# A fused two-layer trunk on one core: PSUM banks of the mLSTM given out anew, its sums of squares taken behind the products of the values, and in the tail the sums of squares one half later

## The chip, the cores and the metric

The kernel runs on one core of one Trainium2 chip. The metric is the device time of one execution in microseconds (us); the median of three runs of the kernel before is 1196.1 us (1193.45 to 1197.48). One more execution was taken under the hardware profiler; all rows of the trace are from that one.

## The reference, cut to what matters

The input is 512 tokens of 1024 channels in float32. Two layers follow each other, and a last norm.

```python
def rmsnorm(x, g):
    y = x * lax.rsqrt(jnp.mean(x * x, axis=-1, keepdims=True) + EPS)
    return y * g

def sqrelu_mlp(h, w1, w2):
    return jnp.square(jax.nn.relu(h @ w1)) @ w2

# layer 0
h = h + diff_attention(rmsnorm(h, attn_norm[0]), ...)
h = h + sqrelu_mlp(rmsnorm(h, mlp_norm[0]), w1[0], w2[0])     # 1024 -> 4096 -> 1024
# layer 1
h = h + mlstm_mixer(rmsnorm(h, mlstm_norm[0]), ...)
h = h + sqrelu_mlp(rmsnorm(h, mlp_norm[1]), w1[1], w2[1])
return rmsnorm(h, final_norm)

def mlstm_mixer(h, ...):
    proj = h @ w_in            # q and k (512 + 512), v 1024, output gate 1024, gates 8
    qk = silu(causal_depthwise_conv(q and k, width 4))
    i_pre, log_f = gates       # 4 heads each; log_sigmoid of the second
    ...                        # scores, decays, values of 4 heads, rmsnorm of each head
    return (sigmoid(o_pre) * ht) @ w_out
```

## The kernel before, in words

Everything lies with channels on the 128 partitions and the 512 tokens along a row: the residual stream is `h[0]` to `h[7]` (two of them in one tile, `h2[0]` to `h2[3]`). A product in float32 is made of three matmuls: each operand is split in a rounded high part (`hi`, ScalarE, `L254`) and the rest (`lo`, VectorE, `L528`; `L513` for the operands of the layers), and `hi*hi`, `lo*hi` and `hi*lo` are summed in PSUM. Weights come in units of 128 rows by 1024 columns: SyncE starts a DMA into one of three `raw` tiles, ScalarE writes `whi`, VectorE writes `wlo`; a unit is requested two units ahead of its use. The MLP's second product goes by a Strassen-like scheme of seven products (`down`, `L922` to `L924`), whose sums are taken out of PSUM by `L937` to `L940` and added to `h` by `L945`.

**Order.** TensorE's instructions stand in the order in which the Python code emits them. Each step of a matrix product calls `tick`, and `after(n, fn)` puts a piece of side work (a norm, a head's scores) `n` ticks behind the place where it is called, so the `T_...` numbers say where in TensorE's order side work stands. On VectorE, ScalarE and GpSimdE a scheduler orders the instructions as the program is built. All engines run their own list strictly in order.

**PSUM** has 8 banks of 512 columns. `idle` holds them with the one that was given out longest ago first. `banks(mm=3, sc=2, ac=3)` gives the first 3 to the tag `mm`, the next 2 to `sc` and the last 3 to `ac`, in the order in which the call names the tags. `bank(tag)` takes a tag's banks in turn.

**The start of the mLSTM.** While `down` for the last rows of `h` (`q` = 3, `i` = 3) is being taken out of PSUM, `mlstm` begins: `vpair_mm(x, 264)` makes the values of head 0 with the gates, 256 + 8 columns, for four blocks of 128 tokens in four banks (one of `mm`, three of `ac`), over eight operands `x[0]` to `x[7]`: 96 matmuls, `L432` to `L434`, 16 ticks. The operands come from `h` by ScalarE (`xh`) and VectorE (`xl`). The norm's factor for each token comes from the sum of squares over the channels: `square_in` squares each `h[k]` (ScalarE) and adds the squares to `acc` (GpSimdE, `L524`); `token_scale`, `T_MRS` ticks after the start, splits `acc`, sums over the partitions by two matmuls (`L535`, `L536`), and takes the reciprocal root: `L559`, then Ln, Exp and Square on ScalarE, then `L552`, `L553` and `L561`, which writes `rs`. `T_GATES` ticks behind the 96 matmuls, `gates` turns `rs` (`L569`), reads the gates (`L1047`, `L1049`) and takes the values out of their four banks (ScalarE, and VectorE's `L582`). Eight tiles of q and k follow (`ntile_mm`, n0 to n7 here: 24 matmuls of 512 columns each, 8 ticks, `L400` to `L402`), which go into the `mm` banks in turn, and are taken out by `evict_qk`: `L1026`, one ScalarE pass, three `L1030` on VectorE, a sigmoid, `L1035` or `L1037`, a split. `T_GROWS` and `T_GCOLS` place the work on the gates' rows and columns. Ln and Exp lie in one of ScalarE's function tables and the sigmoid in another; changing it is `L245`. Then come the heads: their scores are `L1106` (decays) and `L1117` to `L1119`, both in the two `sc` banks.

**The tail.** `finish` makes the last two rows of tiles of the output, `h[6]` and `h[7]` (`j` = 0, 1), for the first 256 tokens and then for the other 256 (`i` = 0, 1): 24 matmuls for each `j` and `i`. `early_sums` splits `acc` (squares of `h[0]` to `h[5]`) and sums it over the partitions by four matmuls, `L1249` and `L1250`; `tail` adds the product to `h` (`L1256`) and squares it; `scaled` adds those two squares (`L1262`), takes the reciprocal root, multiplies `h` by it (`L1272`) and starts the DMAs to the output. The last norm's weights and a factor of -0.5 are put on `h` beforehand (`L1253`, `L1258`).

Of the kernel before, what the change touches and what calls it, by code (L numbers as in the profile page):

```python
# [14 lines left out]
AF = mybir.ActivationFunctionType  # L15
ALU = mybir.AluOpType
# [6 lines left out]
KT = D // P  # L23
# [11 lines left out]
C_AN, C_M0, C_MN, C_M1, C_FN, C_HN, C_SUB, C_CW, C_CB = 0, 8, 16, 24, 32, 40, 48, 49, 81  # L35
# [22 lines left out]
T_M, T_H = 15, 22  # L58
D_MLS = [(5, 8, 6), (5, 7, 9), (5, 9, 10), (7, 8, 12)]

T_GATES, T_GROWS, T_GCOLS, T_MRS = 3, 22, 56, 9
T_SIG = 2

T_MLP = 11
# [121 lines left out]
def trunk(ctx: ExitStack, tc, xT, wgt, wgt2, cols, rows, rel, consts, outT):  # L186
# [18 lines left out]
    def banks(**tags):  # L205

        free = list(idle)
        for tag, n in tags.items():
            turn[tag], free = free[:n], free[n:]
# [15 lines left out]
    mm = nc.tensor.matmul  # L225
    vec = nc.vector
    pool = nc.gpsimd
# [22 lines left out]
    def act(out, x, func, **kw):  # L250
        name = {AF.Exp: LNSET, AF.Ln: LNSET, AF.Sigmoid: SGSET}.get(func)
        if name:
            tables(name)
        ins = nc.scalar.activation(out, x, func, **kw)  # L254
        if name:
            behind(ins, loaded["load"])
            loaded["uses"].append(ins)
# [238 lines left out]
    def col(c):  # L496
        return colt[:, c : c + 1]
# [17 lines left out]
            square_in(k, acc)  # L515
        return lambda: (hi, lo)

    def square_in(k, acc):
        if k == 0:
            act(acc, h[k], AF.Square)  # L520
        else:
            s = tmp()
            act(s, h[k], AF.Square)
            pool.tensor_tensor(acc, acc, s, op=ALU.add)  # L524

    def split(src, hi, lo, eng=None):
        act(hi, src, AF.Copy)
# [35 lines left out]
    def scale_tile(name):  # L563
        return cp.tile([P, T], F32, tag=name, name=nm(name))
# [276 lines left out]
    def mlp(x, acc, g0, finish=None):  # L841
        with ExitStack() as st:
# [49 lines left out]
            def down(q, i):  # L892
# [53 lines left out]
                for n in (2 * i, 2 * i + 1):  # L946
                    if g0 is not None:
                        nxt.append(operand(n, g0, nacc))
                    else:
                        if n == 0:  # L950
                            finish.acc = acc_tile()
                        square_in(n, finish.acc)

            after(T_MLP, lambda: token_scale(acc, rs))
            ps = group_mm(x)
# [24 lines left out]

    def mlstm(x, acc):
        with ExitStack() as st:
            banks(mm=3, sc=2, ac=3)
            gp = Buffers(tc, st, name="gp", bufs=1)
            qp = Buffers(tc, st, name="qp", bufs=16)
            sg = Buffers(tc, st, name="sg", bufs=8)
# [248 lines left out]
    def finish(operands):  # L1235
# [10 lines left out]
        def early_sums():  # L1246
            split(acc, sh, sl)
            for s, c in zip(stat, (slice(0, H), slice(H, T))):
                mm(s[:, :H], ones_d, sh[:, c], start=True, stop=False)  # L1249
                mm(s[:, :H], ones_d, sl[:, c], start=False, stop=False)  # L1250

        for k in range(KT - 2):
            vec.tensor_scalar(h[k], h[k], col(C_FN + k), -0.5, op0=ALU.mult, op1=ALU.mult)  # L1253

        def tail(n, c, s):
            vec.tensor_tensor(h[n][:, c], part[n - pair[0]][:, c], h[n][:, c], op=ALU.add)  # L1256
            act(s, h[n][:, c], AF.Square)
            vec.tensor_scalar(h[n][:, c], h[n][:, c], col(C_FN + n), -0.5, op0=ALU.mult, op1=ALU.mult)  # L1258

        def scaled(c, stat, ss):  # L1260
            for s in ss:
# [16 lines left out]
        for i, c in enumerate((slice(0, H), slice(H, T))):  # L1278
            ss = [tmp()[:, :H] for _ in pair]
            for j, n in enumerate(pair):  # L1280
                hi, lo = units[j]
                for k in range(KT):
                    w = slice(k * P, (k + 1) * P)
                    a, b = operands(k, i)
                    mm(part[j][:, c], hi[:, w], a, start=k == 0, stop=False)
                    mm(part[j][:, c], hi[:, w], b, start=False, stop=False)
                    mm(part[j][:, c], lo[:, w], a, start=False, stop=k == KT - 1)
                    tick()
                tail(n, c, ss[j])
                if i == 0 and j == 0:  # L1290
                    early_sums()
            if i == 0:
                after(T_FIN, lambda c=c, ss=ss: scaled(c, stat[0], ss))
            else:
                scaled(c, stat[1], ss)
# [94 lines left out]
```

## Time and profile before

| | |
|---|---|
| median of 3 runs | 1196.1 us (1193.45 to 1197.48) |
| the profiled execution | 1194.34 us, of which the span from first to last instruction 1192.3 us |
| TensorE matmuls | 1147.5 us busy, 96% of the span |
| VectorE | 919.9 us, 77% |
| ScalarE | 603.0 us, 51% |
| GpSimdE | 189.2 us, 16% |
| granted TensorE clock, mean | 0.983 |

Reading: matmuls are pipelined, so each row's duration (0.28 us for 256 columns) is longer than the distance to the next one's start (0.12 us); the distance is what counts. A row of the timeline gives the start, the duration, the engine, the line, what is written and read, and in brackets how long the engine sat idle ahead of it and what released it. In the view by windows, each stretch has its length, then busy microseconds and instructions of TensorE's matmuls (PE), its weight loads, VectorE (DVE), ScalarE (ACT) and GpSimdE (POOL), the clock granted to TensorE as a share of full speed, the share of the DMA engines and what they moved.

### The profile page before, as it was taken

Reading aid. Unit: us, or ns where it says so; the run is one execution under the profiler, and the core shown is the slowest. Engines: PE = TensorE matmul, PEld = TensorE weight load, DVE = VectorE, ACT = ScalarE, POOL = GpSimd, SP = SyncE. Lnnn points to the kernel's source line nnn. Section 1 sums busy time; section 2 is a strip of 40 time slices with the busy share of each in tenths; the row PEclk is TensorE's granted clock in tenths of the full one; section 3 lists DMA queues with packets and bytes.
Section 4 is the critical chain, followed back from the end, with each engine's and each line's share of the span. In section 5 each row is a group of like instructions: output and inputs, shape, how many; then the busy total and the mean of one; then the engine's idle time right before and its main releaser. Section 6 shows DMA issues by size and latency. Waiting matters only on the chain.

```text
span 1192.3 us, 17221 instructions
## 1 busy us (share of the span) xinstructions
PE 1147.5 (96%) x6730; PEld 1011.2 (85%) x6730; DVE 919.9 (77%) x1387; ACT 603.0 (51%) x909; POOL 189.2 (16%) x180
## 2 busy tenths in 40 slices
PE   7899999999999999999989899999999999999994
PEld 5778888888998998989877789888889889899894
DVE  7789888587967957867989857766697686786884
ACT  5577776564534534434544537654453353443441
POOL 4432332130000000000221312223000000000011
PEclk9899999999999999999989999999999999999997
DMA  6622222233263362461222221223325526426312
GB/s 202 198 71 71 75 85 71 71 124 111 66 190 112 89 176 89 111 191 53 83 71 70 76 83 54 57 85 107 110 84 136 171 67 162 139 67 185 89 32 71
DMA packets 36592, 123.91 MB, mean 104 GB/s; under 512 B 4351, under 2 KB 6418, under 8 KB 36512
## 3 DMA queue, kind: packets, MB, share of 16 engines
q1 hardware_dynamic: 30288, 103.38, 27.0%
q0 software_dynamic: 5104, 17.87, 7.7%
q10 hardware_dynamic: 1120, 1.57, 0.4%
q8 instruction: 53, 0.87, 0.3%
q14 instruction: 27, 0.22, 0.1%
HBM read 108.11 MB, written 4.74 MB: 95 GB/s over the span
## 4 chain that ended last, share of the span: by engine, by line
PE 78%; DVE 14%; ACT 3%; issue 3%; DMA 2%; POOL 1%; DVEq 0%; SPq 0%; POOLq 0%; ACTq 0%
PE bank L401 15%; PE bank L402 15%; PE bank L400 15%; PE bank L923 7%; PE bank L924 7%; PE bank L922 7%; DVE wlo L528 2%; PE bank L432 2%; PE bank L433 1%; PE bank L434 1%; DVE tmp_tmp L1030 1%; DMA raw<-wgt 1%; DVE x_xl L513 1%; PE bank L730 1%; ACT whi L254 1%
## 5 line engine op out<-in xcount | busy, mean ns | idle before, releaser
L402 PE MATMUL bank<-x_xh,wlo 128*128 128x512 f32 x640 | 255.4, 399 | 1.3 <-DVE wlo L528 1.3
L401 PE MATMUL bank<-x_xl,whi 128*128 128x512 f32 x640 | 254.8, 398 | 1.0 <-DVE x_xl L513 1.0
L400 PE MATMUL bank<-x_xh,whi 128*128 128x512 f32 x640 | 254.0, 397 | 1.4 <-ACT whi L254 1.4
L254 ACT ACTIVATE whi<-raw 128x1024 fp32r<-128x1024 f32 (+2 forms) x128 | 133.4, 1042 | 120.9 <-PE bank L923 48.1
L528 DVE TENSOR_TENSOR wlo<-raw,whi 128x1024 fp32r<-128x1024 f32 (+2 forms) x128 | 161.9, 1265 | 35.2 <-ACT whi L254 34.6
L922 PE MATMUL bank<-uh,whi 128*128 128x256 f32 x560 | 157.9, 282 | 0.0
L924 PE MATMUL bank<-uh,wlo 128*128 128x256 f32 x560 | 157.8, 282 | 0.0
L923 PE MATMUL bank<-ul,whi 128*128 128x256 f32 x560 | 157.8, 282 | 0.0
L400 PEld LDWEIGHTS bank<-x_xh,whi 128*128 128x128 f32 x640 | 122.8, 192 | 28.8 <-ACT whi L254 2.1
L402 PEld LDWEIGHTS bank<-x_xh,wlo 128*128 128x128 f32 x640 | 121.1, 189 | 29.3 <-DVE wlo L528 2.4
L401 PEld LDWEIGHTS bank<-x_xl,whi 128*128 128x128 f32 x640 | 121.5, 190 | 28.3 <-DVE x_xl L513 1.4
L922 PEld LDWEIGHTS bank<-uh,whi 128*128 128x128 f32 x560 | 106.0, 189 | 0.1
L923 PEld LDWEIGHTS bank<-ul,whi 128*128 128x128 f32 x560 | 105.7, 189 | 0.3
L924 PEld LDWEIGHTS bank<-uh,wlo 128*128 128x128 f32 x560 | 105.8, 189 | 0.0
L943 POOL DMA_DIRECT2D h<-work x24 | 20.8, 866 | 511.1 <-DVE work L940 391.5
L254 ACT ACTIVATE uh<-chains 128x1792 fp32r<-128x1792 f32 (+1 forms) x35 | 55.6, 1590 | 57.8 <-DVE chains L883 57.7
L528 DVE TENSOR_TENSOR ul<-chains,uh 128x1792 fp32r<-128x1792 f32 (+1 forms) x35 | 66.0, 1886 | 23.7 <-ACT uh L254 23.4
L524 POOL TENSOR_TENSOR acc_acc<-acc_acc,tmp_tmp 128x512 f32<-128x512 f32 x33 | 54.6, 1654 | 170.8 <-ACT tmp_tmp L254 169.7
L432 PE MATMUL bank<-whi,x_xh 128*128 128x256 f32 (+1 forms) x256 | 73.9, 289 | 7.1 <-DVE work L939 5.7
L876 DVE SCALAR_TENSOR_TENSOR tmp_tmp<-bank,rs_rs 128x512 f32<-128x512 f32 x64 | 44.1, 689 | 45.9 <-PE bank L402 45.5
L254 ACT ACTIVATE whi<-wsums 128x1024 fp32r<-128x1024 f32 x47 | 49.8, 1059 | 51.5 <-PE bank L923 30.3
L433 PE MATMUL bank<-wlo,x_xh 128*128 128x256 f32 (+1 forms) x256 | 73.0, 285 | 0.0
(302 smaller groups left out, 2669.6 us busy)
## 6 DMA issues: line engine op xcount, KB each, us to landing
raw<-wgt SPq DMA_DIRECT2D x156, 512.0 KB, 3.7
rawx<-wgt SPq DMA_DIRECT2D x32, 512.0 KB, 4.2
h<-work POOLq DMA_DIRECT2D x24, 512.0 KB, 5.8
skew<-frd POOLq DMA_DIRECT2D x8, 320.0 KB, 7.3
bias_bias<-skew POOLq DMA_DIRECT2D x8, 256.0 KB, 3.1
outT<-h SPq DMA_DIRECT2D x6, 256.0 KB, 2.5
raw<-wgt SPq DMA_DIRECT2D x2, 528.0 KB, 3.6
h<-xT ACTq DMA_DIRECT2D x4, 256.0 KB, 4.9
```

The costliest lines, as they stand in the source:

```text
L254: ins = nc.scalar.activation(out, x, func, **kw)
L400: mm(ps, whi, x[0], start=first, stop=False)
L401: mm(ps, whi, x[1], start=False, stop=False)
L402: mm(ps, wlo, x[0], start=False, stop=last)
L432: mm(ps, xh, hi[:, c], start=k == 0, stop=False)
L433: mm(ps, xh, lo[:, c], start=False, stop=False)
L524: pool.tensor_tensor(acc, acc, s, op=ALU.add)
L528: (eng or vec).tensor_tensor(lo, src, asf(hi), op=ALU.subtract)
L876: vec.scalar_tensor_tensor(m, p, 0.0, rs, op0=ALU.max, op1=ALU.mult)
L922: mm(out[name], hi[:, n], uh[:, t], start=first, stop=False, skip_group_check=late)
L923: mm(out[name], hi[:, n], ul[:, t], start=False, stop=False, skip_group_check=late)
L924: mm(out[name], lo[:, n], uh[:, t], start=False, stop=k == 3, skip_group_check=late)
```

## The change

Four edits:

1. The mLSTM's banks are given out in the order `ac`, `mm`, `sc` instead of `mm`, `sc`, `ac`.
2. Four places in the mLSTM's start: `token_scale` 22 ticks after the start instead of 9, `gates` 14 ticks behind the 96 matmuls instead of 3, the rows at 30 instead of 22, the columns at 60 instead of 56.
3. In the tail, `early_sums` stands behind the second `j` of the first half instead of the first, and the squares of `h[4]` and `h[5]` are added to `acc` by VectorE instead of GpSimdE.
4. Also in the tail, the weights of the last norm times -0.5 are made once (`gain`), and `h[0]` to `h[5]` are scaled by them on ScalarE instead of VectorE.

```diff
-T_GATES, T_GROWS, T_GCOLS, T_MRS = 3, 22, 56, 9
+T_GATES, T_GROWS, T_GCOLS, T_MRS = 14, 30, 60, 22
...
-    def square_in(k, acc):
+    def square_in(k, acc, eng=None):
         if k == 0:
             act(acc, h[k], AF.Square)
         else:
             s = tmp()
             act(s, h[k], AF.Square)
-            pool.tensor_tensor(acc, acc, s, op=ALU.add)
+            (eng or pool).tensor_tensor(acc, acc, s, op=ALU.add)
...
-                        square_in(n, finish.acc)
+                        square_in(n, finish.acc, vec if i == 2 else pool)
...
-            banks(mm=3, sc=2, ac=3)
+            banks(ac=3, mm=3, sc=2)
...
+        gain = scale_tile("rs2")[:, :KT]
+        vec.tensor_scalar(gain, colt[:, C_FN : C_FN + KT], -0.5, None, op0=ALU.mult)
         for k in range(KT - 2):
-            vec.tensor_scalar(h[k], h[k], col(C_FN + k), -0.5, op0=ALU.mult, op1=ALU.mult)
+            act(h[k], h[k], AF.Copy, scale=gain[:, k : k + 1])
...
-            vec.tensor_scalar(h[n][:, c], h[n][:, c], col(C_FN + n), -0.5, op0=ALU.mult, op1=ALU.mult)
+            vec.tensor_scalar(h[n][:, c], h[n][:, c], gain[:, n : n + 1], None, op0=ALU.mult)
...
-                if i == 0 and j == 0:
+                if i == 0 and j == 1:
                     early_sums()
```

Below are three places of the built programs, with the engine's instructions in their order. Lines from 1253 on have numbers larger by 2 in the changed kernel.

First, TensorE at the start of the 96 matmuls of `vpair_mm` (the four blocks of tokens go in four banks; the names end in the bank's number, 77 to 84). The first matmul of each block before:

```order
L432 MATMUL bank_80<-whi_91,x_xh_129 128x264
L432 MATMUL bank_84<-whi_91,x_xh_129 128x264
L432 MATMUL bank_82<-whi_91,x_xh_129 128x264
L432 MATMUL bank_83<-whi_91,x_xh_129 128x264
```

and of the change:

```order
L432 MATMUL bank_77<-whi_91,x_xh_129 128x264
L432 MATMUL bank_80<-whi_91,x_xh_129 128x264
L432 MATMUL bank_81<-whi_91,x_xh_129 128x264
L432 MATMUL bank_79<-whi_91,x_xh_129 128x264
```

VectorE's `L937` to `L940` of the last `down` read banks 84, 83 and 82 in both kernels; those now go to `mm`'s last place and to `sc`.

Second, ScalarE from the split of `acc` for the mLSTM's norm on (`sh` is the high part of `acc`, `chains` the tile of Ln, Exp and Square, `whi` a weight unit's high part, `vh` the values', `tmp<-conv` the first pass of `evict_qk`). Before:

```order
L254 ACTIVATE sh_sh_332<-acc_acc_128 128x512
L254 ACTIVATE whi_91<-raw_88 128x1024
L254 ACTIVATE chains<-chains 128x512 x3
L254 ACTIVATE whi_89<-raw_86 128x1024
L254 ACTIVATE vh_0_v_5227<-bank_80,rscol_rscol_472 128x256
```

and of the change:

```order
L254 ACTIVATE sh_sh_332<-acc_acc_128 128x512
L254 ACTIVATE whi_89<-raw_86 128x1024
L254 ACTIVATE chains<-chains 128x512
L254 ACTIVATE whi_90<-raw_87 128x1024
L254 ACTIVATE chains<-chains 128x512
L245 ACT_TABLE_LOAD
L254 ACTIVATE chains<-chains 128x512
L254 ACTIVATE tmp_tmp_255<-conv_5080,colt 128x512
L254 ACTIVATE vh_0_v_5276<-bank_77,rscol_rscol_472 128x256
```

The three passes of the reciprocal root now have a split of weights and a change of table between them; the table is changed 10 times in the whole program instead of 8 (the first load apart).

Third, the tail on VectorE, from the last step of `down` that it takes out of PSUM on (`h_96` is `h[2]` and `h[3]`, `h_97` is `h[4]` and `h[5]`, `h_98` is `h[6]` and `h[7]`). Before:

```order
L937 TENSOR_TENSOR work<-bank_80,work 128x2x256
L1253 TENSOR_SCALAR h_96<-h_96,colt 128x512
L938 TENSOR_TENSOR work<-bank_82,work 128x512
L939 TENSOR_TENSOR work<-bank_81,work 128x512
L940 TENSOR_TENSOR work<-bank_82,work 128x256
L945 TENSOR_TENSOR h_97<-h_97,work 128x1024
L1256 TENSOR_TENSOR h_98<-bank_78,h_98 128x256
L1253 TENSOR_SCALAR h_97<-h_97,colt 128x512 x2
L1258 TENSOR_SCALAR h_98<-h_98,colt 128x256
L528 TENSOR_TENSOR sl_sl_333<-acc_acc_128,sh_zeros 128x512
```

and of the change:

```order
L937 TENSOR_TENSOR work<-bank_77,work 128x2x256
L938 TENSOR_TENSOR work<-bank_81,work 128x512
L939 TENSOR_TENSOR work<-bank_78,work 128x512
L940 TENSOR_TENSOR work<-bank_81,work 128x256
L945 TENSOR_TENSOR h_97<-h_97,work 128x1024
L1258 TENSOR_TENSOR h_98<-bank_83,h_98 128x256
L524 TENSOR_TENSOR acc_acc_128<-acc_acc_128,tmp_tmp_204 128x512
L524 TENSOR_TENSOR acc_acc_128<-acc_acc_128,tmp_tmp_233 128x512
L1260 TENSOR_SCALAR h_98<-h_98,rs_0_rs_336_2325 128x256
L528 TENSOR_TENSOR sl_sl_333<-acc_acc_128,sh_zeros 128x512
```

The six scalings have left VectorE, and two adds have come. On TensorE the four matmuls of `early_sums` stood behind 24 matmuls of the first half, and now stand behind 48.

## The prediction, made before the run

> **What bounds the kernel now.** I read the page first, then who waited for whom on TensorE, then the stretches around its long waits.
>
> ```profile
> span 1192.3 us, 17221 instructions
> PE 1147.5 (96%) x6730; PEld 1011.2 (85%) x6730; DVE 919.9 (77%) x1387; ACT 603.0 (51%) x909; POOL 189.2 (16%) x180
> ```
>
> TensorE (PE) is busy for 96% of the span, so time is gained only where it stands still or runs slowly. Its waits (in all, times, longest):
>
> ```profile
> PE bank L432 <- DVE work L939: 5.7, 1, 5.7
> PE bank L1249 <- ACT sh_zeros L254: 5.1, 1, 5.1
> PE bank L1106 <- ACT e_e L254: 3.9, 1, 3.9
> ```
>
> The first is the start of the mLSTM, the second the tail, the third lies 80 us behind the first, where the heads' scores begin. The change touches the first two. In the view by windows each of them costs more than the wait:
>
> ```profile
> 593.11:596.52 3.41, 1.61 (x12) 1.19 (x10) 3.28 (x4) 2.88 (x5) 0.44 (x1) 1.00 0.64 234
> 596.52:606.76 10.24, 4.90 (x22) 4.90 (x23) 10.14 (x16) 2.92 (x6) 4.69 (x4) 0.50 0.28 90
> 606.76:610.17 3.41, 3.41 (x29) 3.41 (x28) 2.74 (x5) 1.34 (x2) 1.62 (x1) 1.00 0.00 0
> 1163.28:1166.69 3.41, 0.00 (x0) 0.00 (x0) 3.12 (x3) 1.16 (x4) 2.82 (x2) 0.98 0.00 0
> 1166.69:1173.52 6.83, 6.19 (x27) 5.89 (x28) 0.69 (x1) 0.45 (x1) 0.00 (x0) 0.51 0.00 0
> ```
>
> The granted clock falls to 0.50 after the wait and stays there for three and for two stretches of 3.41 us. Ahead of the first fall TensorE had been busy for 1.61 of 3.41 us: half a stretch of idleness is enough here. The second row also shows VectorE (DVE) busy for 10.14 of 10.24 us while TensorE waits. That decides what the first wait is worth.
>
> **The tail (edits 3 and 4).** In order of time, as now:
>
> ```profile
> 1157.07 1.27 DVE L1253 TENSOR_SCALAR h<-h,colt 128x512 f32<-128x512 f32 x3
> 1159.05 0.28 PE L1285 MATMUL bank<-uh,whi 128*128 128x256 f32 x1
> 1160.49 0.69 DVE L939 TENSOR_TENSOR work<-bank,work 128x512 f32<-128x512 f32 x1
> 1161.55 1.22 DVE L945 TENSOR_TENSOR h<-h,work 128x1024 f32<-128x1024 f32 x1
> 1161.79 0.28 PE L1287 MATMUL bank<-uh,wlo 128*128 128x256 f32 x1
> 1162.80 1.46 ACT L254 ACTIVATE tmp_tmp<-h 128x512 f32<-128x512 f32 x3 [4.46 <-DVE h L945]
> 1163.57 2.90 POOL L524 TENSOR_TENSOR acc_acc<-acc_acc,tmp_tmp 128x512 f32<-128x512 f32 x2 [2.63 <-ACT tmp_tmp L254]
> 1166.51 0.63 ACT L254 ACTIVATE sh_zeros<-acc_acc 128x512 fp32r<-128x512 f32 x1 [2.25 <-POOL acc_acc L524]
> 1167.19 0.58 PE L1249 MATMUL bank<-sh_zeros,ones_d 128*128 128x256 f32 x1 [5.12 <-ACT sh_zeros L254]
> 1173.65 0.28 PE L1285 MATMUL bank<-sh_sh,whi 128*128 128x256 f32 x1
> ```
>
> The first 24 matmuls run from 1159.05, 0.12 us apart; the next could start at 1161.91. The sums wait for `acc`: `h[4]`, `h[5]` at 1162.77, two adds on GpSimdE (2.90 us), the split (0.63). Then the other 24 matmuls run at half clock, and the second half starts at 1173.65: 11.74 us behind 1161.91.
>
> With the change: four of the six scalings no longer stand ahead of `L945`, so `L939` starts when its products end, 1159.05 - 0.12 + 0.28 = 1159.2, and `L945` ends about 1.2 us earlier, at 1161.5. Squares end by 1162.7; the adds, now on VectorE at 0.69 each (bounded by `L939`, of the same size), by 1163.8. On ScalarE the split of `acc` now stands behind two scalings (nearest row, its square of 128x512: 1.46 for three, of which one is half as wide, so 0.6 each) and the first small square: it runs from 1164.3 to 1165.0, and VectorE's `sl` ends at 1165.7. TensorE goes straight on with the 24 matmuls to 1164.8, so the wait left is 0.2 for `sh` and 0.7 for `sl`. With the last three small matmuls the second half starts at 1166.05: **7.6 us earlier**. Bounds: if `L945` comes no earlier, 1.2 us later everywhere, 6.4; if GpSimdE still at work on the squares of `h[2]`, `h[3]` slows VectorE's adds as it did in the mLSTM (below), 6.0; with no wait at all, 8.3. [...] From the second half on both kernels have the same order, and `scaled`'s waits keep their distance from its start; the scalings on ScalarE end by 1164.3, six instructions of 0.6 in idle time. If that cover fails, each costs its 0.6 in front of `sh`.
>
> **The start of the mLSTM (edits 1 and 2).**
>
> ```profile
> 593.56 0.29 PE L432 MATMUL bank<-whi,x_xh 128*128 128x264 f32 x1
> 601.86 0.59 PE L432 MATMUL bank<-whi,x_xh 128*128 128x264 f32 x1 [5.68 <-DVE work L939]
> 602.17 1.23 DVE L945 TENSOR_TENSOR h<-h,work 128x1024 f32<-128x1024 f32 x1
> 603.43 0.72 ACT L254 ACTIVATE x_xh<-h,colt 128x512 fp32r<-128x512 f32 x1 [6.36 <-DVE h L945]
> 604.25 0.75 DVE L513 SCALAR_TENSOR_TENSOR x_xl<-h,colt,x_xh 128x512 fp32r<-128x512 f32 x1
> 605.12 3.32 POOL L524 TENSOR_TENSOR acc_acc<-acc_acc,tmp_tmp 128x512 f32<-128x512 f32 x2 [5.21 <-ACT tmp_tmp L254]
> 605.52 1.77 DVE L513 SCALAR_TENSOR_TENSOR x_xl<-h,colt,x_xh 128x512 fp32r<-128x512 f32 x1
> 610.23 0.40 PE L536 MATMUL bank<-sl_sl,ones_d 128*128 128x512 f32 x1
> 611.70 0.68 DVE L559 TENSOR_SCALAR chains<-bank 128x512 f32<-128x512 f32 x1
> 615.55 0.39 PE L400 MATMUL bank<-x_xh,whi 128*128 128x512 f32 x1
> 615.78 0.40 PE L401 MATMUL bank<-x_xl,whi 128*128 128x512 f32 x1
> 615.86 0.43 DVE L561 TENSOR_SCALAR rs_rs<-chains 128x512 f32<-128x512 f32 x1
> 619.53 0.48 DVE L582 SCALAR_TENSOR_TENSOR vl_v<-bank,rscol_rscol,vh_v 128x256 fp32r<-128x256 f32 x1
> 621.07 1.28 ACT L245 ACT_TABLE_LOAD   x1
> 622.37 1.06 ACT L254 ACTIVATE whi<-raw 128x1024 fp32r<-128x1024 f32 x1
> ```
>
> The wait for `L939`'s bank goes. Next late is the operand: `h[6]` is ready at 603.40, its `xh` at 604.15, the `xl` of `h[7]` at about 607.5 (VectorE's second `L513` takes 1.77 beside GpSimdE's add, the one ahead of it 0.75). TensorE reaches `k` = 6 at 593.56 + 72 x 0.121 = 602.3 and ends the 96 matmuls at 608.7, not at 615.5. That is 6.8 us ahead, and it is given back in two waits. (A matmul of 512 columns starts 0.233 us behind the one before: 615.55, 615.78, and so on.) (a) `L536` now stands 18 matmuls of 0.233 into n0, and ends at 613.5, 3 us later than now. `rs` took 5.7 us from there; to these come the split of a unit that waits for n0's end (615.2 to 616.3, 1.06) and a change of table (1.28): `rs` at 620.7 where it was 616.3, and `L569`, due at 619.0, waits 1.7. (b) n2 needs the bank of the first values, whose `L582` now stands behind `L1026`, the small gate rows and three `L1030`: 625.4, and n2, due at 622.5, waits 2.9. n2 ends at 631 where it ended at 633.
>
> What counts is the end of this stage:
>
> ```profile
> 609.14:679.89 70.75, 63.75 (x96) 1.00 0.25 75
> 633.30:679.89 46.59, 45.20 (x62) 1.00 0.23 68
> 678.59 0.40 PE L402 MATMUL bank<-x_xh,wlo 128*128 128x512 f32 x1
> 682.86 0.69 PE L1106 MATMUL bank<-gs,sel 128*128 128x384 f32 x1 [3.87 <-ACT e_e L254]
> 684.55 0.69 PE L1117 MATMUL bank<-qk_qkh,qk_qkh 128*128 128x384 f32 x1 [1.00 <-DVE e_e L1120]
> ```
>
> The two window rows are VectorE's alone: from 609.14 to 679.89 it is idle for 7.0 us, of them 1.4 in the last 46.6. TensorE gets to `L1106` at 678.8 and waits for that backlog. So the stage ends when VectorE has done the same 63.75 us of work, and the question is its idle time: with the change 2.1 for `L536`, 2.1 for the unit's split, 1.4 for the table and Square, about 2.0 in four waits for ScalarE behind the other tables and splits, and 1.4 as now at the end: 9.0. It starts 0.5 earlier (a weights' split takes the place of the wait for `acc`), and one of GpSimdE's adds, each of which slows it by about 1 us, falls in idle time (0.6). Sum: 9.0 - 7.0 - 0.5 - 0.6 = +0.9. The two new waits, 4.6 us within 6.5, should bring the clock to half in n2, as 1.8 us did at 596.52: some 2.4 us on TensorE, half of it passed on to VectorE through the next split, +1.2. Against that stands a smaller wait at `L1106` with less at half clock behind it, -1.0. I take **+1.1 us**, with -2 (the backlog shrinks by two of the four small waits and the clock holds) and +4 (two stretches at half clock, all passed on) as ends. DMAs of weights are asked for earlier; at a share of 0.25 they have room. The four edits of places on SyncE and GpSimdE move no queue past another.
>
> [...]
>
> **The sum.** 1194.3 - 7.6 + 1.1 = 1187.8 for a profiled execution. The one shown is 1.8 below the median of the runs, so against that median: 1196.1 - 6.5 = **1189.6**.
>
> **Rivals.** A difference of 0.3%, 3.6 us, is about what a measurement can tell from none.
>
> 1. *TensorE keeps its lead in the mLSTM.* If VectorE's backlog isn't what `L1106` waits for but TensorE's own pace, the 6.8 us stay, less the 2.4 us of half clock: 1196.1 - 7.6 - 4.4 = 1184.1. For it: n2 ends 2 us earlier in my own reckoning. Against: the 1.4 us of idle time in 46.6. 0.13.
> 2. *The clock holds through the new waits.* Then the stage gives 0.9 - 1.0 = -0.1, and the time is 1196.1 - 7.7 = 1188.4. Against it the row at 593.11. 0.12.
> 3. *The tail gives less and the mLSTM costs more.* `sl` late by 2 us, the clock at half for one stretch of the second half (1.7), and +4 in the mLSTM: 1196.1 - 7.6 + 1.2 + 1.7 + 4 = 1195.4, no change that can be told. 0.13.
> 4. *Slower: the mLSTM's tiles stay at half clock.* [...] At a clock of 0.50 a tile of 24 takes up to 11.2 us instead of 5.6, less the 4 us of slack ahead of `L1106`. From three tiles on (16.8 - 4 = 12.8) it outweighs the tail by over 3.6 us: 1201 there, 1218 with all six. Against it: the clock came back within three stretches, with VectorE as full. 0.05.
>
> The forecast itself has 0.57.
>
> **How the numbers follow.** The forecast's own range is 1186.5 (mLSTM -2) to 1193.7 (mLSTM +4, tail -6.4), and 1.5 us more on both sides for runs of one kernel that differ by 4. To hold 8 in 10 it reaches down to rival 1 and up to most of rival 3: 1184 to 1195.5. Below 1192.5 lie rivals 1 and 2 and nearly all of the forecast (0.54): 0.79; above 1199.7 rival 4: 0.05; between, the rest: 0.16.
>
> **What would show it.** Tail: `L1249` with a wait under 1 us and no half clock behind it; from the first matmul of `finish` to its second half 7.0 us instead of 14.6. mLSTM: no wait for `L937` or `L939`; small ones for `x`; waits at `L569` (1.7) and at n2's first `L400` (2.9, for `vl`), half clock behind them; VectorE idle for 3.5 us or more between `acc`'s split and `rs`; `L1106`'s second row at 683 to 685. The prediction is wrong if VectorE reaches the heads much earlier or later, or if the tail's `sh` waits for more than its two scalings.

## The result, and the profile after

The changed kernel takes **1188.0 us** (median of 4 runs, 1187.0 to 1189.0) against 1196.3 for the kernel before on the same chip (4 runs, 1193.5 to 1197.5). The ratio of the runs is 0.9934, with a 95% interval from 0.9914 to 0.9955: faster by 0.45 to 0.86%, some 8 us. The profiled execution took 1188.99 us.

First the page of the changed kernel, span and busy time, then TensorE's waits (in all, times, longest):

```profile
span 1187.3 us, 17224 instructions
...
PE 1144.2 (96%) x6730; PEld 1006.3 (85%) x6730; DVE 915.3 (77%) x1384; ACT 608.5 (51%) x917; POOL 184.6 (16%) x178
```

```profile
PE bank L730 <- DVE vl_v L582: 5.8, 2, 3.9
PE bank L400 <- DVE vl_v L582: 3.3, 2, 2.5
PE bank L1106 <- ACT e_e L254: 2.3, 1, 2.3
PE bank L569 <- DVE rs_rs L561: 2.0, 2, 1.2
PE bank L536 <- DVE sl_sl L528: 1.9, 1, 1.9
PE bank L432 <- ACT x_xh L254: 1.8, 1, 1.8
...
PE bank L1087 <- DVE ig L1077: 1.5, 1, 1.5
```

The first row lies in the first layer, 53 to 58 us from the start, where both kernels have the same instructions; it was 3.1 us before and says nothing of the change. The two waits of over 5 us at one place (`L939`'s bank, `sh` of the tail) are gone. In their place stand four new ones of 1.2 to 2.5 us at the start of the mLSTM: for `x[6]` (`L432`), at `L569`, at n2 (2.5 of the second row; `vl` is the low part of the values) and at `L1087`, the last three on VectorE. (`L536`'s 1.9 was there before.) `L1106` waits 2.3 instead of 3.9.

The tail, in order of time (start, duration, engine, line, what is written and read, idle time ahead):

```profile
1161.31 0.28 PE L1287 MATMUL bank<-uh,whi 128*128 128x256 f32 x1
...
1162.66 1.28 DVE L945 TENSOR_TENSOR h<-h,work 128x1024 f32<-128x1024 f32 x1
...
1164.71 1.49 DVE L524 TENSOR_TENSOR acc_acc<-acc_acc,tmp_tmp 128x512 f32<-128x512 f32 x2
...
1165.04 1.32 ACT L254 ACTIVATE h<-h,rs_rs 128x512 f32<-128x512 f32 x2
...
1166.57 0.61 ACT L254 ACTIVATE sh_zeros<-acc_acc 128x512 fp32r<-128x512 f32 x1
...
1167.96 0.38 PE L1250 MATMUL bank<-sl_sl,ones_d 128*128 128x256 f32 x1 [0.34 <-DVE sl_sl L528]
...
1168.42 0.28 PE L1287 MATMUL bank<-sh_sh,whi 128*128 128x256 f32 x1
```

From the first matmul to the second half 7.11 us instead of 14.60, with 0.34 us of waiting. The start of the mLSTM:

```profile
595.73 0.29 PE L432 MATMUL bank<-whi,x_xh 128*128 128x264 f32 x1
...
606.43 0.39 PE L432 MATMUL bank<-whi,x_xh 128*128 128x264 f32 x1 [1.81 <-ACT x_xh L254]
...
612.07 0.68 DVE L528 TENSOR_TENSOR sl_sl<-acc_acc,sh_sh 128x512 fp32r<-128x512 f32 x1
...
617.07 0.69 DVE L559 TENSOR_SCALAR chains<-bank 128x512 f32<-128x512 f32 x1 [2.32 <-PE bank L536]
...
619.40 1.23 DVE L528 TENSOR_TENSOR wlo<-raw,whi 128x1024 fp32r<-128x1024 f32 x1 [1.64 <-ACT whi L254]
...
623.32 0.43 DVE L561 TENSOR_SCALAR rs_rs<-chains 128x512 f32<-128x512 f32 x1
...
628.40 0.50 PE L400 MATMUL bank<-x_xh,whi 128*128 128x512 f32 x1 [2.54 <-DVE vl_v L582]
...
686.20 0.44 PE L1106 MATMUL bank<-gs,sel 128*128 128x384 f32 x1 [2.34 <-ACT e_e L254]
```

TensorE, VectorE, ScalarE and GpSimdE have the same instructions in the same order ahead of 595.73 as before, yet the mLSTM starts there and not at 593.56: over the 14 profiles of this study that start lies between 592.4 and 597.4. So each section is counted below from its own start: the mLSTM's from its first `L432`, the tail's from the first matmul of `finish`. So counted, the stage's end (the second row of `L1106`) stands at 90.47 us where it stood at 89.30, the tail begins at 565.58 where it began at 565.49, and from there to the end of the span it takes 25.99 us where it took 33.25. **All of the gain in this profile is the tail's.**

### The profile page after: what moved, and what is told of

Read it like the earlier page. It is cut to its first block, busy times and chain, and to the rows that moved or that the text cites. A ratio compares the mean times of both kernels' runs of the same rounds, so it can differ in the third digit from the quotient of the medians.

```text
span 1187.3 us, 17224 instructions
## 1 busy us (share of the span) xinstructions
PE 1144.2 (96%) x6730; PEld 1006.3 (85%) x6730; DVE 915.3 (77%) x1384; ACT 608.5 (51%) x917; POOL 184.6 (16%) x178
## 3 DMA queue, kind: packets, MB, share of 16 engines
q1 hardware_dynamic: 30288, 103.38, 27.6%
## 4 chain that ended last, share of the span: by engine, by line
PE 77%; DVE 14%; ACT 4%; issue 2%; DMA 2%; POOL 0%; DVEq 0%; SPq 0%; ACTq 0%; POOLq 0%
PE bank L401 15%; PE bank L402 15%; PE bank L400 15%; PE bank L923 8%; PE bank L924 8%; PE bank L922 8%; DVE wlo L528 2%; DVE tmp_tmp L1030 1%; PE bank L434 1%; PE bank L433 1%; PE bank L432 1%; DMA raw<-wgt 1%; DVE x_xl L513 1%; ACT whi L254 1%; PE bank L730 1%
## 5 line engine op out<-in xcount | busy, mean ns | idle before, releaser
L524 POOL TENSOR_TENSOR acc_acc<-acc_acc,tmp_tmp 128x512 f32<-128x512 f32 x31 | 51.7, 1668 | 168.0 <-ACT tmp_tmp L254 167.0
L432 PE MATMUL bank<-whi,x_xh 128*128 128x256 f32 (+1 forms) x256 | 73.3, 286 | 1.8 <-ACT x_xh L254 1.8
L434 PE MATMUL bank<-whi,x_xl 128*128 128x256 f32 (+1 forms) x256 | 73.0, 285 | 0.8 <-DVE x_xl L513 0.7
```

The source lines that it names most:

```text
L432: mm(ps, xh, hi[:, c], start=k == 0, stop=False)
L434: mm(ps, xl, hi[:, c], start=False, stop=k == KT - 1)
L524: (eng or pool).tensor_tensor(acc, acc, s, op=ALU.add)
```

## The experiments

Each ratio is against the kernel before, run beside on the same chip (its median there lay between 1195.1 and 1197.9 us, so ratios compare better than medians). The four columns of distances are from one profile of each kernel, in us.

| kernel | start of mLSTM to `L1106` | to the tail | tail to its second half | tail to the end | median | ratio (95%) |
|---|---|---|---|---|---|---|
| before | 89.30 | 565.49 | 14.60 | 33.25 | 1196.3 | |
| changed | 90.47 | 565.58 | 7.11 | 25.99 | 1188.0 | 0.9934 (0.9914 to 0.9955) |
| edits 3 and 4 alone | 88.87 | 566.31 | 7.17 | 25.97 | 1189.2 | 0.9938 (0.9921 to 0.9955) |
| edit 3 alone | 88.87 | 565.94 | 8.27 | 28.38 | 1191.3 | 0.9959 (0.9943 to 0.9975) |
| sums later alone | 89.47 | 565.96 | 9.70 | 30.09 | 1191.9 | 0.9959 (0.9945 to 0.9973) |
| edits 1 and 2 alone | 87.87 | 562.85 | 14.46 | 33.16 | 1194.0 | 0.9978 (0.9964 to 0.9993) |
| edit 1 alone | 91.38 | 567.12 | 14.32 | 32.99 | 1198.0 | 1.0009 (0.9999 to 1.0020) |
| waits filled | 88.31 | 564.12 | 7.12 | 25.90 | 1187.6 | 0.9927 (0.9914 to 0.9939) |
| VectorE heavier | 95.89 | 572.27 | 7.15 | 26.76 | 1193.1 | one run |
| VectorE lighter | 87.94 | 560.78 | 7.13 | 25.97 | 1183.3 | one run |
| sums at 20 | 88.70 | 563.94 | 7.14 | 26.00 | 1186.1 | 0.9913 (0.9900 to 0.9927) |
| shorter chain | 87.87 | 563.14 | 7.15 | 25.92 | 1186.4 | 0.9924 (0.9909 to 0.9939) |
| adds on VectorE, filled | 85.33 | 558.72 | 7.12 | 26.02 | 1182.0 | 0.9890 (0.9874 to 0.9906) |
| adds on VectorE | 87.98 | 561.52 | 7.15 | 26.03 | 1183.2 | 0.9876 (0.9860 to 0.9893) |

### The tail alone (edits 3 and 4)

The changed kernel with edits 1 and 2 taken back:

```diff
-T_GATES, T_GROWS, T_GCOLS, T_MRS = 14, 30, 60, 22
+T_GATES, T_GROWS, T_GCOLS, T_MRS = 3, 22, 56, 9
...
-            banks(ac=3, mm=3, sc=2)
+            banks(mm=3, sc=2, ac=3)
```

> The kernel before with edits 3 and 4 alone (the tail); the mLSTM as before. Theory (all of the gain lies in the tail): from the first matmul of the tail to its second half 7.0 to 7.2 us instead of 14.6, no half clock there; time 7.5 us under the kernel before (about 1188.8), so the same as the changed kernel within 1 us; in the mLSTM the waits of before stand (5.7 us for L939's bank, 3.9 us at L1106). Rival (part of the gain comes from the mLSTM): the time lies 2 us or more above the changed kernel's, at 1190 or more.

7.17 us, and the ratio is the changed kernel's (0.9938 and 0.9934). In the mLSTM the waits of before stand (5.70 and 3.88 us). The tail alone makes the gain of the changed kernel, as far as these ratios can tell them apart.

### The mLSTM's start alone (edits 1 and 2)

The kernel before with these two edits:

```diff
-T_GATES, T_GROWS, T_GCOLS, T_MRS = 3, 22, 56, 9
+T_GATES, T_GROWS, T_GCOLS, T_MRS = 14, 30, 60, 22
...
-            banks(mm=3, sc=2, ac=3)
+            banks(ac=3, mm=3, sc=2)
```

> The kernel before with edits 1 and 2 alone (the start of the mLSTM); the tail as before. Theory (the lead of 6.8 us is given back within the stage, since VectorE's backlog sets its end): time within 1.5 us of the kernel before, about 1196.4; the second row of L1106 stands 1.0 to 1.5 us later, counted from the first L432, its wait is 1.5 us shorter, and from the first L432 to the first matmul of the tail 565.5 us, as before. Rival (TensorE keeps its lead): 4 us faster, 1192.

Between the two: 2.6 us faster by the ratio (0.8 to 4.3, which shuts out neither the 1.5 nor the 4). In the profile the theory's later end is missed: the stage's end stands 1.43 us *earlier* than before, and the tail is reached 2.6 us earlier. The instructions from the first `L432` to `L1106` are the same as in the changed kernel, and so are the first waits of TensorE, in order of time:

```profile
604.72 0.39 PE L432 MATMUL bank<-whi,x_xh 128*128 128x264 f32 x1 [1.83 <-ACT x_xh L254]
...
620.99 0.66 PE L569 MATMUL bank<-ident,rs_rs 128*128 128x128 f32 x4 [1.22 <-DVE rs_rs L561]
...
625.59 0.50 PE L400 MATMUL bank<-x_xh,whi 128*128 128x512 f32 x1 [2.55 <-DVE vl_v L582]
```

1.83, 1.22, 2.55, against 1.81, 1.21, 2.54 above. What differs is the clock. By windows, first the changed kernel (length, then busy time of TensorE's matmuls, their weight loads, VectorE, ScalarE, GpSimdE; granted clock; DMA), then the kernel with edits 1 and 2 alone:

```profile
605.43:608.84 3.41, 1.67 (x11) 1.47 (x12) 3.38 (x11) 2.38 (x4) 1.51 (x1) 1.00 0.02 5
608.84:612.26 3.42, 3.39 (x16) 3.09 (x15) 3.42 (x5) 0.63 (x1) 1.93 (x2) 0.50 0.00 0
...
625.91:629.32 3.41, 0.92 (x4) 0.79 (x5) 3.37 (x11) 3.13 (x5) 0.00 (x0) 1.00 0.00 0
629.32:632.73 3.41, 3.41 (x10) 2.62 (x9) 3.21 (x8) 3.37 (x7) 1.28 (x1) 0.50 0.01 2
```

```profile
600.83:604.24 3.41, 2.05 (x17) 1.84 (x16) 3.31 (x6) 0.55 (x2) 0.00 (x0) 1.00 0.14 55
604.24:607.66 3.42, 2.21 (x14) 1.81 (x14) 3.42 (x10) 2.08 (x4) 1.97 (x2) 1.00 0.01 2
...
621.31:624.72 3.41, 1.73 (x10) 1.12 (x7) 3.30 (x11) 2.94 (x5) 0.00 (x0) 1.00 0.00 0
624.72:628.13 3.41, 2.54 (x11) 2.09 (x12) 3.17 (x12) 3.18 (x8) 0.56 (x1) 1.00 0.00 0
```

The falls of the granted clock lie whole numbers of 3.41 us apart (the last section has the count), and the waits fall in these stretches as they happen to. In the changed kernel's profile the last 1.0 us of the wait for `x[6]` and the 0.74 for `x[7]` fall in one stretch (busy 1.67 us, then half clock through n0, which puts `L536`, `rs` and all behind it off by 1.1 us), and the wait of n2 lies whole in another. In the other profile a boundary leaves 1.35 us of the wait for `x[6]` in the stretch ahead, and another cuts the wait of n2 in two: three of the four stretches were busy for 2.05 us or more, and the clock also held behind the fourth, busy for 1.73, and on to 662 us. The same instructions of this stage, then, have its end at 87.9 or at 90.5 in these two profiles, by where the waits fall.

### The waits filled

The changed kernel with matmuls of a zero weight in its waits:

```diff
+            gap = w > 256 and k == KT - 2 and tb == 0
+            for _ in range(14 if gap else 0):
+                mm(ps, zero_w, hi[:, c], start=False, stop=False)
             mm(ps, xh, hi[:, c], start=k == 0, stop=False)
             mm(ps, xh, lo[:, c], start=False, stop=False)
+            for _ in range(5 if gap else 0):
+                mm(ps, zero_w, hi[:, c], start=False, stop=False)
...
+            def busy(n):
+                for _ in range(n):
+                    mm(turn["sc"][0], zero_w, x[0]()[0], start=True, stop=True)
...
             def gates(psv):
+                busy(4)
...
             def gate_cols():
+                busy(5)
...
+                if hd == 1:
+                    busy(10)
                 evict_qk(hd, ntile_mm(x))
```

> The changed kernel, with matmuls of a zero weight put where TensorE waits at the start of the mLSTM (14 and 5 around the wait for x[6], 4 ahead of L569, 10 ahead of n2, 5 ahead of L1087), each group shorter than the wait it stands in, so that TensorE does not go idle there. They add zeros or write a bank that is overwritten. Theory (whether these waits, each under 2.6 us, bring the clock to half is a matter of where they fall in the 3.41-us stretches; half clock at n0 is what put the stage's end at 90.5 us behind the first L432 in the changed kernel, against 87.9 in the kernel with edits 1 and 2 alone, where the same waits of the same lengths fell otherwise): no half clock between the first L432 and L1106, whose second row stands 87.9 us behind the start within 0.7; time 1 to 2.5 us under the changed kernel, 1186 to 1187. Rival (the difference between the two is something else): 90.5 and 1188 as in the changed kernel.

By window, the whole way from the first `L432` to `L1106`:

```profile
597.38:685.69 88.31, 82.46 (x459) 69.53 (x457) 78.41 (x119) 45.72 (x68) 20.19 (x14) 1.00 0.26 78
```

The clock is 1.00 throughout, and the stage's end 88.31 (expected 87.9 within 0.7), with 38 matmuls more. The time misses the 1186 to 1187 expected: 1187.6 can't be told from the changed kernel's. The profile shows that the clock holds with the waits filled; what that is worth over many runs stays open.

### Edit 1 alone

The kernel before with the banks in the new order:

```diff
-            banks(mm=3, sc=2, ac=3)
+            banks(ac=3, mm=3, sc=2)
```

> The kernel before with edit 1 alone: banks in the new order, but the sums of squares still 9 ticks after the start. Theory: the wait of 5.7 us for L939's bank goes, and L535, which now stands 54 matmuls in (reached some 6.6 us after the start), waits for the split of acc, some 15 us after the start: a wait of 7 to 9 us there, with half clock behind it; VectorE gets its data no earlier, so L1106 stands where it did within 1 us, and the time is that of the kernel before within 1.5 us. Rival (the order of banks by itself is worth something): over 3 us faster or slower.

```profile
PE bank L535 <- ACT sh_sh L254: 9.1, 1, 9.1
PE bank L1106 <- ACT e_e L254: 3.9, 1, 3.9
```

These are TensorE's two longest waits between 590 and 700 us, where the mLSTM starts: the 5.7 us for a bank became 9.1 for `acc`, and nothing was won (ratio 1.0009). The stage's end stands 2.1 us later than before (91.38 for 89.30), where within 1 us was expected; why stays open. Edit 1 is of no use without edit 2; edit 2 without edit 1 was not run.

### VectorE heavier and lighter

The changed kernel with eight more products of 0.75 us (by a factor of zero), and with eight fewer; the second leaves out a tap of the convolution, so it computes something else and serves for its time alone:

```diff
                 for j in range(3):
                     vec.scalar_tensor_tensor(y, xs[:, 1 + j : 1 + j + T], col(C_CW + 4 * tile_i + j), y,
                                              op0=ALU.mult, op1=ALU.add)
+                vec.scalar_tensor_tensor(y, xs[:, 1 : 1 + T], zero_f, y, op0=ALU.mult, op1=ALU.add)
```

```diff
-                for j in range(3):
+                for j in range(2):
```

> The changed kernel with a fourth product added to each of the eight tiles of q and k in evict_qk, of the size of L1030 and with a factor of zero: 8 more of 0.75 us on VectorE, 6.0 us, all ahead of the second row of L1106. Theory (VectorE's backlog sets the stage's end): that row stands 5 to 6 us later, at 93 to 96.5 us behind the first L432 (87.9 to 90.5 without). Rival (TensorE's pace sets it): less than 2 us later, since L1106 waits only 1.3 to 2.3 us.

> The changed kernel with the last of the three products L1030 left out in each of the eight tiles of q and k (the convolution then has three taps): 8 of 0.75 us, 6.0 us less on VectorE ahead of the second row of L1106. Theory (VectorE's backlog sets the stage's end): the waits at L1106, for wlo and at L1087 go, and the row stands 4 to 6 us earlier, 82 to 86 us behind the first L432. Rival (TensorE's pace): the wait at L1106 goes (1.3 to 2.3 us) and nothing else.

Windows from the first `L432` to the second row of `L1106`: the changed kernel, then heavier, then lighter.

```profile
595.73:686.20 90.47, 78.72 (x421) 66.13 (x419) 78.96 (x119) 45.80 (x68) 20.07 (x14) 0.96 0.26 77
```

```profile
592.37:688.26 95.89, 80.52 (x420) 67.33 (x418) 86.08 (x130) 47.53 (x70) 18.95 (x13) 0.94 0.25 78
```

```profile
594.85:682.79 87.94, 79.12 (x421) 67.63 (x419) 75.80 (x114) 48.12 (x71) 22.34 (x14) 0.94 0.27 83
```

6.0 us more put the stage's end off by 5.4 us, and the run by about as much: VectorE sets it, and 5.2 us are waited there instead of 2.3. (One stretch more at half clock, at 653 us, may have a part in it.) 6.0 us less bring it forward by only 2.5, a miss: with the wait at `L1106` gone, TensorE's own pace sets the end, with three stretches at half clock. (What VectorE no longer has to do comes out behind: the tail is reached 4.8 us earlier.) So VectorE's backlog is the bound of the changed kernel, but a thin one: 2.5 us under it lies TensorE's. Both kernels were run once.

### The chain to `rs` shortened

The changed kernel, first with the sums at 20 ticks; then also the gates at 12, and the square of the root on VectorE, which waits there anyway, instead of ScalarE behind its change of table (1.28 us).

```diff
-T_GATES, T_GROWS, T_GCOLS, T_MRS = 14, 30, 60, 22
+T_GATES, T_GROWS, T_GCOLS, T_MRS = 14, 30, 60, 20
```

```diff
-T_GATES, T_GROWS, T_GCOLS, T_MRS = 14, 30, 60, 22
+T_GATES, T_GROWS, T_GCOLS, T_MRS = 12, 30, 60, 20
...
-        act(a, y, AF.Square)
+        if on_vec:
+            vec.tensor_tensor(a, y, y, op=ALU.mult)
+        else:
+            act(a, y, AF.Square)
...
-            after(T_MRS, lambda: token_scale(acc, rs))
+            after(T_MRS, lambda: token_scale(acc, rs, True))
```

> The changed kernel with the sums of squares 20 ticks after the start instead of 22: L536 two ticks (1.4 us) earlier, still behind the rest of acc, and the split of a weight unit (1.04 us) out of the chain of Ln, Exp and Square. Theory (the chain to rs is where the lead is given back): rs (L561) 2.4 us earlier, 24.1 to 25.2 us behind the first L432 instead of 26.5 to 27.6; L569 does not wait, n2's first L400 waits 0.1 to 1.4 instead of 2.5; stage's end 1 to 2.4 us earlier and the time 1 to 2 us under the changed kernel. Rival (VectorE's work alone counts, its idle time moves elsewhere): rs earlier, but the second row of L1106 where it was within 0.5.

> The changed kernel with the sums of squares at 20 ticks instead of 22, gates at 12 instead of 14, and in the mLSTM's norm the square of the root on VectorE (0.69 us, where it now idles 1.2) instead of ScalarE behind the change of table (1.28 + 0.63). Theory (the chain to rs is where the lead is given back): rs 2.4 + 1.2 us earlier than in kernels of the same clock, 23 us behind the first L432 with full clock there, up to 26 with two stretches at half; n2's wait for vl under 1.5 us; stage's end (second row of L1106) 87 to 88 us behind the start; time 2 to 3 us under the changed kernel, about 1185.5. Rival (VectorE's amount of work alone counts): stage's end and time as in the changed kernel.

`rs` came 27.4 and 25.0 us behind the start (27.6 in the changed kernel): over 2 us later than expected in the first, where two stretches at half clock (one in the changed kernel) fell on the last of the 96 matmuls and n0, and where VectorE's split of a weight unit (1.22 us) now stands between `L553` and `L561`. The second has the two stretches as well and lies in its expected range. `L569` waits for nothing in either; n2 still waits 2.6 and 1.6. The stage's end is 1.8 and 2.6 us earlier, of which the clock alone could make that much. The times, 1186.1 and 1186.4, lie under the changed kernel's 1188.0, but the intervals overlap: a gain of 1 to 2 us is likely, and not shown.

### The adds off GpSimdE

The changed kernel with sums at 18 ticks, gates at 10, the square on VectorE as above, and the last two adds of squares of the mLSTM's norm on VectorE; with the filled waits for `x[6]` and ahead of `L1087`, and without.

```diff
-T_GATES, T_GROWS, T_GCOLS, T_MRS = 14, 30, 60, 22
+T_GATES, T_GROWS, T_GCOLS, T_MRS = 10, 30, 60, 18
...
-            square_in(k, acc)
+            square_in(k, acc, vec if g0 == C_MN and k >= KT - 2 else None)
```

> The changed kernel with sums at 18 ticks, gates at 10, the square of the root on VectorE, the last two adds of squares of the mLSTM's norm on VectorE instead of GpSimdE, and zero-weight matmuls in the waits for x[6] (14 and 5) and ahead of L1087 (5). Theory: the rest of acc 2 us earlier (two adds of 0.7 instead of 3.3 for two), rs 21 to 22 us behind the first L432, no half clock between the first L432 and L1106; but VectorE has 1.4 us of adds and 0.7 of the square more, so the stage's end stays at 86 to 88 us; time 1184 to 1186. Rival (nothing beyond the kernel with the earlier chain alone): the same time as that one within 0.7 us.

> The kernel of 1182 us (sums at 18 ticks, gates at 10, the square of the root and the last two adds of squares on VectorE) without the zero-weight matmuls. In that kernel VectorE was idle for 5.4 us from the first L432 to the second row of L1106 (11.5 in the changed kernel), TensorE did not wait at that row, and no stretch at half clock lay in the first 60 us. Theory 1 (the adds on VectorE and the earlier chain make the gain, by less idle time of VectorE; the zero-weight matmuls only keep the clock): stage's end 85 to 88 us behind the start, later where a stretch at half clock falls into the first 20 us; time 1182 to 1184.5. Theory 2 (the clock is what counts): half clock in n0 as in the kernel with the earlier chain alone, stage's end 88 us and time 1185 to 1187.

VectorE in order of time, first the changed kernel, then the one without filled waits:

```profile
607.94 1.77 DVE L513 SCALAR_TENSOR_TENSOR x_xl<-h,colt,x_xh 128x512 fp32r<-128x512 f32 x1
609.64 1.36 DVE L474 TENSOR_SCALAR gs<-ones_f 128x256 fp32r<-128x256 f32 x1
```

```profile
605.96 0.74 DVE L513 SCALAR_TENSOR_TENSOR x_xl<-h,colt,x_xh 128x512 fp32r<-128x512 f32 x1
606.62 0.68 DVE L524 TENSOR_TENSOR acc_acc<-acc_acc,tmp_tmp 128x512 f32<-128x512 f32 x1
```

Beside one of GpSimdE's last two adds (1.84 and 1.61 us) the same `L513` takes 1.77, without it 0.74: the add cost VectorE about 1.0 us, more than the 0.68 that it takes on VectorE itself. So VectorE ends up with the same work, two adds and a square more included, and `acc` comes earlier (its split 13.8 us behind the start instead of 15.2):

```profile
593.55:681.53 87.98, 79.04 (x421) 67.49 (x419) 78.95 (x122) 46.12 (x68) 19.25 (x12) 0.94 0.26 79
```

```profile
593.96:679.29 85.33, 79.82 (x444) 68.30 (x443) 79.93 (x123) 46.30 (x68) 19.28 (x12) 0.98 0.26 82
```

Those are the stage's windows without and with filled waits. VectorE is busy for 78.95 us as in the changed kernel (78.96), but idle for 9.0 instead of 11.5, and for 5.4 with the waits filled. TensorE waits at the second row of `L1106` in neither. Without filled waits that row itself stands no earlier than with the shorter chain (87.98 and 87.87), both with two stretches at half clock in n0; what is won shows behind it, at the tail (561.52 for 563.14). Both beat the changed kernel and their intervals lie wholly under its own: 0.9876 (0.9860 to 0.9893) without, 0.9890 (0.9874 to 0.9906) with. The filled waits leave one stretch at half clock of three in the profile (stage's end 85.3 for 88.0), but bring nothing that these runs can tell, so theory 1 has it. The adds were not moved without the earlier chain, so their own share is not shown. The best kernel of this study is the one without filled waits, 5 us (by the medians) to 7 (by the ratios) under the changed kernel.

### The tail in its parts

The kernel before with the sums moved alone:

```diff
-                if i == 0 and j == 0:
+                if i == 0 and j == 1:
                     early_sums()
```

> The kernel before with the sums of squares behind the second row of tiles (j = 1) alone: the adds of the last two squares stay on GpSimdE, the six scalings on VectorE. From the rows of before acc is split at 1167.1 and its rest ready at about 1167.9, while TensorE ends the 48 matmuls at 1164.8. Theory: L1249 waits about 2.3 us and L1250 0.7; second half 5.0 us earlier than before if the clock holds, 3.4 us earlier if it falls to half for one stretch of 3.41 us (TensorE would be busy for some 45% of the stretch with the wait, as in the one that fell at 593). So 1191.3 or 1193. Rival (the place of the sums is all that matters, the adds and scalings nothing): 7.5 us earlier, 1188.8.

and edit 3 whole, with the adds on VectorE, without edit 4:

> The kernel before with edit 3 alone (sums of squares one half later, the last two adds of squares on VectorE); the six scalings stay on VectorE ahead of L945. Theory (the prediction's bound for L945 no earlier: everything 1.2 us later): from the first matmul of the tail to its second half about 8.3 us (7.1 in the changed kernel, 9.7 with the sums moved alone, 14.6 before); L1249 waits 1.0 to 1.4 us, and the clock stays full ahead of the second half; time 6.3 us under the kernel before. Rival (moving the scalings brings nothing, since the adds alone take the wait away): 7.1 us and 7.5 us under. Rival (the adds on VectorE bring nothing): 9.7 us.

TensorE's rows of the sums moved alone, then of edit 3 whole:

```profile
1168.08 0.58 PE L1249 MATMUL bank<-sh_zeros,ones_d 128*128 128x256 f32 x1 [2.28 <-ACT sh_zeros L254]
```

```profile
1168.20 0.39 PE L1249 MATMUL bank<-sh_zeros,ones_d 128*128 128x256 f32 x1 [0.99 <-ACT sh_zeros L254]
...
1169.13 0.39 PE L1250 MATMUL bank<-sl_sl,ones_d 128*128 128x256 f32 x1 [0.54 <-DVE sl_sl L528]
```

Both as worked out: waits of 2.28 and 0.99 us for `sh`, and 9.70 and 8.27 us to the second half (expected 9.6 and 8.3). Both also bring the clock to half behind the sums, which the expectation had for the first only: there the stretch from 1164.38 was busy for 1.42 of 3.41 us, in the second the one from 1166.49 for 1.88. From the tail to the end of the span the moved sums bring 3.2 us (33.25 to 30.09), the adds on VectorE 1.7 more (28.38) and the scalings on ScalarE 2.4 more (25.97). In the timed runs the three steps stand at 0.9959, 0.9959 and 0.9938 (edits 3 and 4), with intervals that overlap: the parts are told by the profiles alone. For edit 3 alone the timed runs gave 4.9 us (3.0 to 6.8), as the 4.9 to the end of the span (33.25 - 28.38); the 6.3 expected is what the profile has up to the second half, into which the half clock then falls. Taken in this order each of the three brings its part, and the last one takes away the wait and the half clock that the first two leave; another order, as the scalings without the adds, was not run.

## Why the prediction was right, and where it was not

**The tail** was right in each step. 7.6 us forecast, 7.49 measured to the second half, 7.26 to the end of the span. `L945` starts 1.35 us behind the first matmul instead of 2.50, 1.15 earlier (forecast 1.2). The two adds take 1.49 us (forecast 1.38), two scalings 1.32 (1.2). No wait of `L1249` was left to speak of (0.2), and `sl` is late by 0.34 instead of 0.7. The bound for `L945` no earlier was 6.4: edit 3 alone gives 14.60 - 8.27 = 6.3. No half clock came, as estimated: the clock is 1.00 from 690.8 to 1178.9 us, with waits of only 0.2 and 0.34 left. In edit 3 alone two waits of 0.99 and 0.54 us were enough for one: their stretch was busy for 1.88 us of 3.41, and the clock was 0.50 behind it.

**The start of the mLSTM** was right in its mechanism. The lead is given back in the waits that were named, `L569` (1.7 forecast, 1.21) and n2 (2.9 forecast, 2.54). `rs` comes 5.3 us later than before, 4.2 with the clock at full (forecast 4.4). That VectorE sets the stage's end is shown by the heavier kernel, so rival 1 falls; rivals 3 and 4 are seen nowhere (in the changed kernel's mLSTM the clock was at half for one stretch at a time). Rival 2's 1188.4 lies nearest to the median, but its condition, a clock that holds, is not met in the changed kernel's profile: behind the stretches at 605.43 and 625.91, busy for 1.67 and 0.92 us, it was 0.50.

**The term of +1.1 us was mis-sized**, and its sign is likely wrong. Counted from the first `L432`, the four kernels with the mLSTM of before reach the tail at 565.49 to 566.31, 565.9 in the mean; the changed kernel at 565.58 (-0.3) and edits 1 and 2 alone at 562.85 (-3.1); timed, the latter gain 2.6 (0.8 to 4.3). Two steps of the prediction made that:

1. *The stage's end without the clock* was +0.9. The kernel that kept its clock there (edits 1 and 2 alone) has -1.43 at `L1106`. Its VectorE, from `sl` to `L1109` (its first work on the heads' scores), and that of the changed kernel:

```profile
610.36:679.23 68.87, 61.25 (x98) 0.98 0.24 77
```

```profile
612.07:683.23 71.16, 61.30 (x97) 0.97 0.25 74
```

   The first window ends behind `L1109`, the second and the prediction's ahead of it; without that instruction's 0.35 us the first has 60.90 us of work in 68.52. So the work fell from 63.75 to 60.9 us, where I had taken off 0.6. A split of weights (1.22) now stands ahead of `sl` instead of behind it, and with it `sl` comes 0.8 later (16.4 us behind the start instead of 15.6), where I had it 0.5 earlier; what makes the other 1.0 us stays open. Idle time was 68.87 - 61.25 = 7.6, not 9.0. The three together give the -1.4: 0.8 - 2.85 + 0.6.

2. *The half clock in n2*, +1.2, stood in the sum whole, with a chance of 0.12 left to a clock that holds. It comes in the changed kernel's profile, with one more in n0 that I had not priced (the waits for `x` stood in the text as small, without a price); both make the 9.9 us of idle time (71.16 - 61.30) and the 2.6 us between the two profiles of this stage. In the other profile neither comes. That term is no number but a draw, here 0 or 2.6.

The last part, a smaller wait at `L1106` with less half clock behind it, was -1.0: the changed kernel has +1.17 at `L1106` and +0.09 at the tail, -1.1.

**The sum**: against the profile before, 1187.8 was forecast and 1188.99 came, of which 2.17 us lie ahead of the mLSTM; without them 1186.8, 1.0 better, the size of the mLSTM's miss in this profile (the tail's 0.3 less and 0.35 us less outside the span cancel). That 1187.8 came so near is in part luck: the mLSTM's miss of 1.0 and the later start of code that the change does not touch, 2.17, have opposite signs. The range for the median, 1184 to 1195.5, had room for both.

## What to carry to other kernels

A wait that is taken off the busiest engine is worth what the next engine's backlog leaves of it: the lead of 6.8 us in the mLSTM brought 0 to 3 by the profiles, while in the tail, where nothing else was late, the 7.5 us arrived. Shorten the work of the engine behind it in the same place (here two adds moved from GpSimdE, which had slowed VectorE by more than they cost it, 1.0 us beside one of them against 0.68, together with an earlier chain to `rs`), and the lead counts. Compare two profiles section by section from a common instruction, with the granted clock beside it, before a difference of 2 us is explained by code.

## What the runs showed of the hardware that was not expected

**Behind which stretches the clock fell.** In every one of the 14 traces the falls of the granted clock lie whole numbers of 3.413 us apart (in the kernel before those at `L1106` and in the tail stand 25.0 and 167.0 stretches behind the one at the start of the mLSTM). Between 100 and 1165 us, with matmuls counted as busy as the profile models them, the clock fell behind 33 stretches, in which TensorE was busy for 0 to 1.90 of 3.41 us; it held behind all 4,281 that were busy for 1.97 or more, and behind six of 1.58 to 1.89. It came back behind stretches busy for 2.87 or more, and never for 2.79 or less. The length of a wait alone does not tell them apart: 1.7 us of waiting within one stretch (605.43 in the changed kernel) cost a stretch at half clock that 2.55 us across a boundary (624.72 in edits 1 and 2 alone) did not. These are counts of the 14 traces; what sets the clock was not measured.

**The same code ahead of the change** (two kernels make a tile of zeros there as well) reached the mLSTM anywhere between 592.4 and 597.4 us, and runs of one kernel differ by up to 6 us (1191.4 to 1197.6 in edits 1 and 2 alone). The clock may make a part of this: the four profiles with three stretches at half clock on record ahead of the mLSTM start it at 595.4 to 597.4 us, the ten with two at 592.4 to 595.7. Waits differ too (`L730`'s 3.1 and 5.8 us above); how much is due to which was not measured.
